# Retention/HGRN2 step on one core: both gates computed token-major in the value phase

## Chip, cores and metric

One of the eight cores of a Trainium2 chip runs the whole kernel. The metric is the device time of one execution in microseconds, as the median of the runs.

## What is computed

One step of a decoder layer for a prompt of 2048 tokens (model width 1024) and eight sample tokens with a past. The input is RMS-normalised and projected to eight groups of 512 columns: query, key, value and gate of the retention branch (rq, rk, rv, rg), and query, forget gate, value and gate of the HGRN2 branch (hq, hf, hi, hgate). Each branch has four heads of width 128. Cut to what matters:

```python
h = rmsnorm(x, norm_g)
rq, rk, rv, rg, hq, hf, hi, hgate = jnp.split(h @ w_in, 8, axis=-1)
rq, rk = rotary(rq, pos), rotary(rk, pos) * RET_DK ** -0.5
o_ret, s_ret_new = chunked_decay_recurrence(rq, rk, rv, log_gamma, s_ret)
o_ret = head_rmsnorm(o_ret, ret_g) * silu(rg)
logf = logaddexp(log(lb), log1p(-lb) + log_sigmoid(hf))
kin = (1 - lb) * sigmoid(-hf)
o_hg, s_hg_new = chunked_decay_recurrence(silu(hq), kin, hi, logf, s_hg)
o_hg = head_rmsnorm(o_hg, hg_g) * silu(hgate)
y = x + concat(o_ret, o_hg) @ w_out      # then the final rmsnorm
```

The recurrence is S_t = diag(f_t) S_{t-1} + k_t v_t^T, o_t = S_t^T q_t. It is worked in chunks of 128 tokens. The new states and the normalised y, for prompt and samples, are the outputs.

## The kernel before

Every float32 product is made of three fp32r products: each operand is split into a high part (a ScalarE copy) and a low part (a VectorE subtraction), in `hi_lo` (L105) and `split` (L109), and high*high, high*low and low*high are accumulated in PSUM. `three` (L303) issues them.

**The value phase.** The values of both branches are computed token-major (tokens on the partitions of the result). Eight pairs of 128-token chunks are worked through in `V_ORDER`. The first two pairs use the eight plain block products; pairs 2 to 7 use the Strassen-Winograd form with seven (`v_pair`, L307, with `PRODUCTS`). For it the weights are summed into T1 to T4 (`wv_comb`) and the tokens into S1 to S4 (`tok_ops`, L259, and `s_split`). `stats` (L222) gets the root mean squares of the tokens, `spread` (L245) brings them across the partitions with small matmuls (prs), and `tok_ops` scales the transposed tokens with them. Seven PSUM banks take the products in turn; ScalarE and VectorE combine them into four 128x512 results per pair (s, u, vo), which are stored to `v_dram`. The work for later pairs is hung behind the products of the current one (`after`).

**The main loop.** There are 16 units: two halves of the tokens, four heads, and for each head an HGRN unit and then a retention unit (`order`, L128). A unit projects a head's columns feature-major: retention q, k and gate (`ret_proj`, L619), HGRN forget gate, q and gate (`hgrn_proj`, L641, and `gate_steps`, L604). `seg_steps` (L564) cuts a projection into segments (512, 256 and 264 tokens in the first half, the eight sample tokens among them; 512 and 512 in the second) and each segment into four steps of six matmuls, followed by the evacuation. The gate is kept as g * silu(gate), features on the partitions (`gt`).

While a unit's projections run, the recurrence of the unit before it is worked off (`ret_rec`, L747; `hgrn_rec`, L781; `tail_steps`, L675). HGRN's steps are three rounds of small score matmuls (`scores0`, `scores`, `scores3`) with updates of k and q on VectorE (L811, L814) and copies on ScalarE (L821, L822) between them; then transposes of k (`kt`), the state sums (`uu`, L690 and L698), the outputs and their norm (`oo`, L705 to L715), and the transposes of the outputs (`tr`, L721), where the gate is multiplied in at L723 before the store to `o_dram`.

**What sets the order.** TensorE's order is the order of the program text; a planner writes it: `merge` (L1071) lays the recurrence's steps between the projection's steps in proportion to hand-written weights:

```python
steps = [(0.3, scores0), (2.3, lambda: scores(1)), (2.3, lambda: scores(3)), (2.3, scores3)]
steps += [(1.9, t["k0"]), (0.9, joined(t["u0"], t["k1"])), (1.1, t["u1"]),
          (1.2, joined(t["o0"], t["o1"])), (2.2, joined(t["t0"], t["t1"])), (0, last)]
```

A projection step weighs its columns/400. The other engines' orders are fixed by the compiler's scheduler; `behind` and `issue_after` tie some instructions to the place where they were written. `side_steps` adds the sample tokens' states (`d_load` to `d_mm`) and the sums of the output weights (`t_load_raw`, `t_sum`, `t_spool`).

**The output phase.** After the main loop the output projection runs, two chunks plainly and seven pairs in the seven-product form.

## Time and profile before

| | |
|---|---|
| median of 3 runs | 1065.55 us (1065.42 to 1066.16) |
| span of the profiled execution | 1062.5 us |
| ScalarE, GpSimd busy in it | 395.3 us, 115.8 us |
| mean granted TensorE clock | 0.999 |
| moved by DMA | 149.64 MB, mean 141 GB/s |
| on the chain that ended last: gate projections (pjg), output pairs (po), value pairs (pv) | 17%, 13%, 11% of the span |

The span runs from the first to the last instruction; the profiled execution is a single one, so its span is compared with the runs' median only through the difference of the two. The page gives the busy time of each engine, the chain of waits that ended last, and the costliest groups of instructions; other views are groups by shape, the timeline in order of time, and the busy time in chosen stretches. PE is TensorE, DVE VectorE, ACT ScalarE, POOL GpSimd. A name such as pjg is the tile that an instruction writes, and L578 the line of the program.

### The profile page before, as it was taken

The numbers are of one execution on the slowest core, as the hardware profiler recorded it, in microseconds if no ns is written. First come the engines' busy times: TensorE is split into PE (matmuls) and PEld (weight loads), VectorE is DVE, ScalarE is ACT, GpSimd is POOL, SyncE is SP. The second block draws the span as 40 slices with busy tenths as digits, with TensorE's granted clock in tenths as the row PEclk, the third lists the DMA queues.
The fourth block names the chain that finished last, engine by engine and source line by source line (L and its number), as shares of the span: only waits on it lengthen the run. The fifth ranks groups of instructions, "written<-read, shape, count | busy, mean of one in ns | idle before, by whom it ended". The sixth has DMA issues, their size and how long they took to land.

```text
span 1062.5 us, 21859 instructions
## 1 busy us (share of the span) xinstructions
PE 1050.9 (99%) x9107; PEld 899.6 (85%) x9107; DVE 733.6 (69%) x1271; ACT 395.3 (37%) x859; POOL 115.8 (11%) x218
## 2 busy tenths in 40 slices
PE   9999999999999999999999999999999999999997
PEld 7788888989989999998988888888788888788775
DVE  6886986594585567457977565746855687678785
ACT  7853323242432243333443323332423244333241
POOL 1110000001000010110110101011010103311122
PEclk9999999999999999999999999999999999999999
DMA  8664346422502240361654235126323337855642
GB/s 303 208 216 156 127 139 225 166 78 100 187 34 80 87 153 2 119 202 39 200 157 122 63 108 151 40 67 182 120 67 109 108 106 268 276 187 200 220 160 99
DMA packets 103890, 149.64 MB, mean 141 GB/s; under 512 B 5872, under 2 KB 69552, under 8 KB 103024
## 3 DMA queue, kind: packets, MB, share of 16 engines
q1 hardware_dynamic: 83888, 110.14, 32.9%
q0 software_dynamic: 6960, 25.24, 6.5%
q10 hardware_dynamic: 12944, 12.88, 3.5%
q8 instruction: 71, 1.16, 0.4%
q14 instruction: 27, 0.22, 0.1%
HBM read 109.86 MB, written 38.37 MB: 140 GB/s over the span
## 4 chain that ended last, share of the span: by engine, by line
PE 91%; DMA 3%; DVE 2%; ACT 2%; issue 1%; POOL 1%; SPq 0%; DVEq 0%; POOLq 0%; ACTq 0%
PE pjg L578 17%; PE po L305 13%; PE pv L305 11%; PE pjkr L578 9%; PE pjqr L578 8%; PE pjqh L578 8%; PE pjfh L578 8%; PE plh L841 2%; DMA xn<-in_x_prompt 2%; PE py L1231 1%; PE pur L690 1%; PE par L757 1%; PE por L705 1%; PE por L707 1%; PE poh L705 1%; PE puh L690 1%
## 5 line engine op out<-in xcount | busy, mean ns | idle before, releaser
L578 PE MATMUL pjg<-xh,w_h 128*128 128x512 f32 (+2 forms) x320 | 113.9, 356 | 0.0
L578 PE MATMUL pjg<-xh,w_l 128*128 128x512 f32 (+2 forms) x320 | 111.3, 348 | 0.0
L578 PE MATMUL pjg<-xl,w_h 128*128 128x512 f32 (+2 forms) x320 | 111.0, 347 | 0.0
L106 ACT ACTIVATE w_h<-wr 128x1024 fp32r<-128x1024 f32 x48 | 50.8, 1059 | 87.5 <-PE pjg L578 33.6
L107 DVE TENSOR_TENSOR w_l<-wr,w_h 128x1024 fp32r<-128x1024 f32 x48 | 58.6, 1222 | 23.3 <-ACT w_h L106 11.4
L578 PEld LDWEIGHTS pjg<-xh,w_l 128*128 128x128 f32 x320 | 60.2, 188 | 7.9
L578 PEld LDWEIGHTS pjg<-xh,w_h 128*128 128x128 f32 x320 | 60.3, 188 | 7.1 <-issue 0.4
L578 PEld LDWEIGHTS pjg<-xl,w_h 128*128 128x128 f32 x320 | 60.3, 188 | 6.7
L578 PE MATMUL pjqr<-xh,w_h 128*128 128x512 f32 (+2 forms) x160 | 58.2, 364 | 0.0
L578 PE MATMUL pjkr<-xh,w_h 128*128 128x512 f32 (+2 forms) x160 | 57.9, 362 | 0.0
L578 PE MATMUL pjfh<-xh,w_h 128*128 128x512 f32 (+2 forms) x160 | 57.4, 359 | 0.0
L821 ACT ACTIVATE kepth<-kh 128x1024 f32<-128x1024 f32 x24 | 25.5, 1062 | 85.6 <-DVE kh L811 85.6
L578 PE MATMUL pjqh<-xh,w_h 128*128 128x512 f32 (+2 forms) x160 | 56.6, 354 | 0.0
L578 PE MATMUL pjfh<-xh,w_l 128*128 128x512 f32 (+2 forms) x160 | 55.7, 348 | 0.0
L578 PE MATMUL pjkr<-xl,w_h 128*128 128x512 f32 (+2 forms) x160 | 55.5, 347 | 0.2 <-issue 0.2
L578 PE MATMUL pjkr<-xh,w_l 128*128 128x512 f32 (+2 forms) x160 | 55.6, 347 | 0.0
L578 PE MATMUL pjqh<-xh,w_l 128*128 128x512 f32 (+2 forms) x160 | 55.6, 347 | 0.0
L578 PE MATMUL pjqr<-xh,w_l 128*128 128x512 f32 (+2 forms) x160 | 55.6, 347 | 0.0
L578 PE MATMUL pjqr<-xl,w_h 128*128 128x512 f32 (+2 forms) x160 | 55.5, 347 | 0.0
L578 PE MATMUL pjqh<-xl,w_h 128*128 128x512 f32 (+2 forms) x160 | 55.5, 347 | 0.0
L578 PE MATMUL pjfh<-xl,w_h 128*128 128x512 f32 (+2 forms) x160 | 55.5, 347 | 0.0
L612 ACT ACTIVATE sg<-pjg 128x512 f32<-128x512 f32 (+2 forms) x40 | 20.4, 510 | 75.9 <-PE pjg L578 65.9
(851 smaller groups left out, 2819.5 us busy)
## 6 DMA issues: line engine op xcount, KB each, us to landing
wr<-in_w_in SPq DMA_DIRECT2D x48, 512.0 KB, 4.8
xn<-in_x_prompt SPq DMA_DIRECT2D x32, 256.0 KB, 3.0
v_dram<-vo SPq DMA_DIRECT2D x32, 256.0 KB, 2.8
v<-v_dram SPq DMA_DIRECT2D x16, 512.0 KB, 4.8
or<-o_dram SPq DMA_DIRECT2D x16, 512.0 KB, 5.8
xro<-in_x_prompt SPq DMA_DIRECT2D x14, 512.0 KB, 3.3
out_y_prompt<-xro POOLq DMA_DIRECT2D x13, 512.0 KB, 3.0
xr<-in_x_t SPq DMA_DIRECT2D x12, 512.0 KB, 4.4
```

The source lines that it names most:

```text
L106: act.activation(h, src, AF.Copy)
L107: dve.tensor_tensor(l, src, h.bitcast(F32), op=ALU.subtract)
L305: pe.matmul(ps, xx, ww, start=(first and n == 0), stop=(last and n == 2))
L578: pe.matmul(ps, ww[:, kk], x[:, k, b0 : b0 + n], start=(k == 0 and i == 0), stop=(k == KT - 1 and i == 2),)
L612: act.activation(sg[:, :n], ps, AF.Sigmoid)
L690: pe.matmul(pu[:, j], ksb[g][:, j], vcol(4 * g + j), start=True, stop=True)
L705: pe.matmul(po[:, j], A[:, c], vcol(c), start=True, stop=src is None)
L707: pe.matmul(po[:, j], qcol(c), src, start=False, stop=True)
L757: pe.matmul(pa[:, j], k[:, cc], q[:, cc], start=True, stop=True)
L821: act.activation(ss[:, 512:], k[:, :HALF], AF.Copy)
L841: pe.matmul(dst[32 * i : 32 * i + 32, c], kk, qq, start=True, stop=True)
L1231: pe.matmul(ps, o[:, kk], w[:, k % 4, i * 512 : (i + 1) * 512], start=(k == 0 and n == 0), stop=(k == KT - 1 and n == 2),)
```

## The change

The gate projections leave the main loop. After the value pairs, the value phase runs through all eight token pairs once more, with the gate columns as weights, in the seven-product form (`TOK`, pairs 8 to 15).

- The scaled tokens and their S sums are stored to DRAM in the first pass (`a_dram`, `s_dram`) and loaded in the second. The first two token pairs, which the first pass handles plainly, are scaled and summed in the second. `x_load` reads the scaled tokens too, so the scaling in `x_split` goes.
- The gate weights are loaded in pairs 3 to 6, multiplied with the sample tokens (`wg_decode`), summed (`w_sums`) and the sums stored (`g_sums`). In pair 7 each weight operand is fetched into the place of the value operand that was last used, and split over pairs 7 and 8.
- A pair now uses three PSUM banks: sums of products accumulate in the bank (`CHAIN`, sign of T4 turned), and copies of intermediate sums are taken by ScalarE.
- The gate results go through sigmoid and product, and to `g_dram`. The recurrence loads them like the values, and multiplies them in token-major, with the norm's factor: four operations of 128x128 in place of one of 128x512. The head norm's weight is applied after the transposes, by ScalarE in place of VectorE.
- The stores of the output weights' sums go from ScalarE's queue to GpSimd's, those of the new sample states from ScalarE's to SP's, one step later.

```diff
-        for g in ((RQ, RK, RG), (HF, HQ, HG))[ty]:
+        for g in ((RQ, RK), (HF, HQ))[ty]:
...
-    V_ORDER = [4, 5, 6, 7, 2, 3, 0, 1]
+    V_ORDER = [4, 5, 6, 7, 0, 1, 2, 3]
+    TOK = V_ORDER + [3, 2, 6, 7, 4, 5, 1, 0]
+    N_V = len(V_ORDER)
...
     def tok_ops(i):
         r0, r1 = xr[i]
...
+            if not spooled(i):
+                sp.dma_start(a_dram[TOK[i]][:, kk], r)
+        if spooled(i):
+            return
...
+        if i < N_V:
+            for n, t in enumerate(sraw[i]):
+                sp.dma_start(s_dram[TOK[i]][n], t)
...
+    CHAIN = [("A11", "B11", "a"), ("A12", "B21", "b"), ("S2", "T2", "a"), ("S1", "T1", "c"),
+             ("S3", "T3", "a"), ("S4", "B22", "c"), ("A22", "T4", "a")]
...
+        def emit(c, ty, ps, plus):
+            o = vq.tile([P, GW], F32, tag="vo", name=f"vo{i}{c}{ty}", bufs=3)
+            if plus:
+                dve.tensor_tensor(o, ps, box[plus], op=ALU.add)
+            elif not gate:
+                act.activation(o, ps, AF.Copy)
+            if gate:
+                src = o if plus else ps
+                sg = vq.tile([P, GW], F32, tag="sg", name=f"sg{i}{c}{ty}")
+                act.activation(sg, src, AF.Sigmoid)
+                dve.tensor_tensor(o, src, sg, op=ALU.mult)
+            v_out(int(gate), c, ty, o)
...
+        for n, (x, w, b) in enumerate(CHAIN):
+            first = b not in banks
+            if first:
+                banks[b] = bank([P, GW], f"pv{i}{b}")
+            ps = banks[b]
             for k in range(4):
-                three(ps, av(i, x, k), wv(w, k), k == 0, k == 3)
+                three(ps, av(i, x, k), wv(w, k), first and k == 0, k == 3, not first)
             if n == 0:
-                act.activation(keep("s1"), ps, AF.Copy)
+                keep("s1", ps)
             elif n == 1:
+                emit(ca, 0, ps, "s1")
             elif n == 2:
+                keep("u2", ps)
             elif n == 3:
+                keep("p5", ps)
             elif n == 4:
+                emit(ca + 1, 1, ps, "p5")
             elif n == 5:
+                emit(ca, 1, ps, "u2")
             else:
+                emit(ca + 1, 0, ps, None)
...
+    def wg_spool(k):
+        for op, r in w_sums(wr[k], wr[k + 4]):
+            sp.dma_start(g_sums[op][:, k], r)
...
+            if op in g_sums:
+                kk = slice(2 * n, 2 * n + 2)
+                r = Bop[op][1][:, kk].bitcast(F32)
+                pool.dma_start(r, g_sums[op][:, kk])
+            else:
+                r = rawp.tile([P, 2, GW], F32, tag="raw", name=f"wg{op}{n}")
+                kk = slice(k0 + 2 * n, k0 + 2 * n + 2)
+                sp.dma_start(r, a["w_g"][kk, :, c0 : c0 + GW].rearrange("k p n -> p k n"))
...
+        if 3 <= i < 7:
+            after[0] += [lambda k=i - 3: wg_load(k)]
+            after[3] += [lambda k=i - 3: wg_decode(k), lambda k=i - 3: wg_spool(k)]
...
-            dve.tensor_tensor(ob[g], po, rs.unsqueeze(2).to_broadcast([P, 4, P]), op=ALU.mult)
+            for j in range(4):
+                dve.scalar_tensor_tensor(
+                    ob[g][:, j], po[:, j], rs[:, j : j + 1], gcol(4 * g + j), op0=ALU.mult, op1=ALU.mult
+                )
...
-            dve.tensor_tensor(
-                ot, pt.rearrange("p a b -> p (a b)"), gt[:, g * 512 : (g + 1) * 512], op=ALU.mult
-            )
+            act.activation(ot, pt.rearrange("p a b -> p (a b)"), AF.Copy, scale=ng[:, hd : hd + 1])
...
-            act.dma_start(t_dram[x, n][:, :, k], y.bitcast(F32).rearrange("p (a b) -> p a b", a=2))
+            pool.dma_start(t_dram[x, n][:, :, k], y.bitcast(F32).rearrange("p (a b) -> p a b", a=2))
...
     def d_mm(hd):
         S, vb = dec["l", hd]
+        ty, h = divmod(hd, NH)
+        sp.dma_start(out[("new_ret_sample", "new_hgrn_sample")[ty]][0, :, h].rearrange("b d v -> d b v"), S)
```

More of the change, by code (lines that the diff above doesn't have):

```diff
@@ L304, in three @@
         for n, (xx, ww) in enumerate(((x[0], w[0]), (x[0], w[1]), (x[1], w[0]))):
-            pe.matmul(ps, xx, ww, start=(first and n == 0), stop=(last and n == 2))
+            pe.matmul(
+                ps, xx, ww, start=(first and n == 0), stop=(last and n == 2), skip_group_check=more
+            )
+    CHAIN = [("A11", "B11", "a"), ("A12", "B21", "b"), ("S2", "T2", "a"), ("S1", "T1", "c"),
+             ("S3", "T3", "a"), ("S4", "B22", "c"), ("A22", "T4", "a")]
     def v_pair(i, after):
-        ca = 2 * V_ORDER[i]
@@ L534, in step_kernel @@
+        if i in (7, 8):
+            for n, (_, op, _) in enumerate(CHAIN):
+                if (n + SPLIT_AT) // 7 == i - 7:
+                    after[(n + SPLIT_AT) % 7] += [lambda op=op: behind(lambda: wg_split(op))]
+        if i == n_tok - 1:
             after[0] += [w_load]
@@ L636, in ret_proj @@
             u[nm] = dst
-        u["gt"], g = gate_steps(half, 0, h)
-        steps.append(g)
         return u, steps
@@ L750, in ret_rec @@
         G = GAMMA[h] ** P
-        vcol = lambda c: v[0][:, c]
+        vcol, gcol = (lambda c, n=n: v[n][:, c] for n in range(2))
         def score(g):
@@ L921, in collect @@
         hd = ty * NH + h
[L922 removed]
+        for dst, key in ((dq, "q"), (dk, "k"), (df, "f")):
             if key in u:
@@ L1109, in unit @@
         box = []
-        steps.insert(len(steps) // 2, (0, lambda: box.append(values(half, ty, h))))
+        steps.insert(len(steps) // 2, (0, lambda: box.extend(values(n, half, ty, h) for n in range(2))))
         return steps, (u, box)
```

240 lines of the change are left out of this document (129 added, 111 removed).

## The prediction

> **What bounds the kernel now.** I read the page first, then the busy time by stage, then the chain that ended last in order of time.
>
> ```profile
> span 1062.5 us, 21859 instructions
> ## 1 busy us (share of the span) xinstructions
> PE 1050.9 (99%) x9107; PEld 899.6 (85%) x9107; DVE 733.6 (69%) x1271; ACT 395.3 (37%) x859; POOL 115.8 (11%) x218
> ```
>
> TensorE (PE) is idle for 1062.5 - 1050.9 = 11.6 us of the whole span. Nothing else comes near it: VectorE (DVE) is at 69%. So the time is the length of TensorE's instruction stream, and a change is worth what it takes out of that stream, less the stops that it brings. The stages show where a stop could come from. Columns: stretch, length, busy time of PE, PEld, DVE, ACT and POOL (instructions), granted clock, share of the DMA engines, GB/s.
>
> ```profile
> 61.85:174.30 112.45, 112.45 (x508) 93.05 (x507) 92.13 (x153) 41.42 (x68) 5.01 (x12) 1.00 0.50 165
> 0.00:20.00 20.00, 18.63 (x109) 14.88 (x109) 11.54 (x25) 13.50 (x27) 0.88 (x8) 1.00 0.88 316
> ...
> 655.40:701.80 46.40, 46.40 (x644) 39.12 (x642) 31.08 (x54) 16.05 (x37) 4.14 (x7) 1.00 0.25 71
> ```
>
> The first row is most of the value phase, the last one unit of the main loop: a retention unit of the second half of the tokens, whose projections run while the recurrence of the HGRN unit before it is worked off. In both TensorE never stops. VectorE is at 92.13/112.45 = 82% and 31.08/46.40 = 67%.
>
> **What TensorE is relieved of and given.** Matmuls are pipelined, so the busy mean of one (403 ns) is not its price. The price is the pitch in the chain.
>
> ```profile
> 61.85 19.09 PE pv L305 x84
> ...
> 185.14 5.44 PE pjg L578 x24
> 190.58 2.84 PE pjfh L578 x24
> ...
> 199.10 2.92 PE pjfh L578 x24
> ```
> ```profile
> L578 PE MATMUL pjg<-xh,w_h 128*128 128x512 f32 x192 | 77.4, 403 | 0.0
> ...
> L578 PE MATMUL pjg<-xh,w_l 128*128 128x264 f32 x64 | 18.3, 285 | 0.0
> L578 PE MATMUL pjg<-xh,w_h 128*128 128x256 f32 x64 | 18.2, 285 | 0.0
> ...
> L403 PE MATMUL pvd<-wvr,pk 128*8 128x256 f32 x64 | 3.8, 379 | 0.0
> ```
>
> Pitches: 5.44/24 = 0.227 us for a projection matmul of 512 columns, 0.118 for 256, 0.122 for 264, and 19.09/84 = 0.227 in the value phase. All eight gate projections (pjg) go. Each group exists for three products (high*high, low*high, high*low), so 3 x 192 x 0.227 + 3 x 64 x 0.118 + 3 x 64 x 0.122 = 130.6 + 22.7 + 23.4 = 176.7 us leave the stream. Eight token pairs of gate products come, of 7 x 12 = 84 matmuls each: 8 x 19.09 = 152.7 us. The gate of the eight sample tokens comes as a second set like pvd, 3.8 us by its row. The spread matmuls stay eight. Sum: 176.7 - 152.7 - 3.8 = **20.2 us less** for TensorE. Part of it is the seventh-for-eighth product; the rest is that the short 256- and 264-column matmuls cost more per column.
>
> **The cover that goes with the gate projections.** A unit's projections are also what TensorE does while VectorE and ScalarE work between two steps of the recurrence. The planner (merge) places the steps by weight over the projections, so with two projections in place of three every gap shrinks to two thirds. In the second half a unit now has 16 steps of six matmuls, 1.36 us each, planner weight 1.28, 20.48 in all. The HGRN steps weigh 14.5 together, so a step whose cumulative weight is c goes out at 0.98 x 20.48/14.5 = 1.38c. The step scores(3) (c = 4.9) follows the sixth matmul step, scores3 (7.2) the eighth: two steps or 2.72 us between them, where there were four. The two transposes (14.5) come two steps behind the outputs (12.3): again 2.72. What these gaps have to hold, from one unit of the second half:
>
> ```profile
> 669.96 0.70 PE L841 MATMUL plh<-qth,kh 128*32 128x16 f32 x62
> ...
> 674.44 0.68 DVE L814 TENSOR_TENSOR qth<-qth,fph 128x512 f32<-128x512 f32 x1
> ...
> 676.27 0.70 PE L886 MATMUL plh<-kepth 128*32 128x32 f32 x32
> ...
> 695.11 0.39 PE L707 MATMUL poh<-sth,qth 128*128 128x128 f32 x2
> ...
> 698.60 0.69 DVE L715 TENSOR_TENSOR obh<-poh,orsh 128x512 f32<-128x512 f32 x1 [1.08 <-POOL orsh L103]
> ...
> 700.80 1.03 PE L721 MATMUL poth<-ident,obh 128*128 128x128 f32 x8
> ```
>
> From the end of scores(3) (670.66) to the second update's end (675.12) it takes 4.46 us; TensorE came 5.61 us later and never noticed. scores3 begins with 0.63 us that need only the older copy (L886), so it must be ready after 2.72 + 0.63 = 3.35: short by 1.1 us. From the last output matmul (695.50) to the second normalised block (699.29) it takes 3.79 us.
>
> That second stretch also grows, because the gate is now applied there: one 128x512 product per block (L715) becomes four of 128x128 with a per-partition factor and a second tensor. The nearest row for one of those is the state update, which has the same operands:
>
> ```profile
> L698 DVE SCALAR_TENSOR_TENSOR sth<-sth,fph,puh 128x128 f32<-128x128 f32 x48 | 16.7, 347 | 9.7 <-PE puh L690 8.3
> ...
> L715 DVE TENSOR_TENSOR obh<-poh,orsh 128x512 f32<-128x512 f32 x16 | 11.1, 691 | 27.7 <-ACT jkh L711 16.9 <-POOL orsh L103 10.8
> ```
>
> 4 x 0.347 - 0.691 = +0.70 us a block, so the block is there 4.49 us after the outputs. The last transposes then end at about 4.49 + 0.28 = 4.77, against 2.72 + 1.03 = 3.75 without a wait: short by 1.0. So 2.1 us for each of the four HGRN recurrences of the second half, 8.4. In the first half the finer segments leave one step of 256 and four of 264 columns in both gaps, 0.71 + 2.92 = 3.63 us. There the same update was ready at 317.77, 4.90 us after its scores (312.87):
>
> ```profile
> 312.17 0.70 PE L841 MATMUL plh<-qth,kh 128*32 128x16 f32 x62
> ...
> 317.08 0.69 DVE L814 TENSOR_TENSOR qth<-qth,fph 128x512 f32<-128x512 f32 x1
> ```
>
> That is short by 4.90 - 0.63 - 3.63 = 0.6 at the scores, and by 4.77 - 3.63 - 1.03 = 0.1 at the transposes: 0.7 x 4 = 2.8. **Main loop: +11.2 us.** Bounds: 0, if VectorE takes the updates ahead of its other work, and 8 x 4.2 = 34, if it always takes them behind one whole rotary evacuation (four operations of the size of L715's, 2.8 us) and a weight split (one of twice that size, at most 1.4). I take the value between because the two measured stretches have that queue as it runs. The gate also lay between the last q evacuation and the next unit's first scores. What stands there now is the transposes (1.03) and one step (1.36), against a sigmoid and two operations of L715's size, about 2 us: cost 0; if those do not cover, 0.5 a unit. Retention recurrences have wider gaps (weights 1.3 and 1.7 of 5.0): 0.
>
> ScalarE takes the transposed blocks in place of VectorE and loses the gate's sigmoids and weight splits; at 16.05/46.40 it stays covered. The stores moved off its queue are costed at nothing. On SP the new-state stores go out one step later, already computed, ahead of weight loads that have a projection's lead (11 us). On POOL a store of the output weights' sums stands ahead of the norm's two operations; if its split is late, it holds them by that split, 1.4 us, and it falls in units with wide gaps.
>
> **The value phase.** It gets eight more pairs, three new kinds of stores, and sums that accumulate in the bank in place of separate banks. So the evacuation of one product must be over before the next but one begins, one product (12 x 0.227 = 2.73 us) later. Now it is far later than that, unnoticed:
>
> ```profile
> 89.21 0.39 PE L305 MATMUL pv<-T1h,s31l 128*128 128x512 f32 x1
> ...
> 99.40 0.68 DVE L334 TENSOR_TENSOR vo<-pv,u 128x512 f32<-128x512 f32 x1
> ```
>
> The fifth product ends at 89.6 and its sum runs at 99.4, behind the next pair's token work. The change relieves that queue: of seven VectorE evacuations a value pair keeps three, the copies go to ScalarE, and the output buffers go from two to three. Walking the queue from the spread (about 1 us after the second product), through eight scalings, two splits, four sums, the first S split and, in pairs 3 to 6, four weight sums, I estimate the add at about 12.3 us after the second product; TensorE asks for it after four more products, a spread and sample matmuls, 10.9 + 1.4. I take 0.5 us for each of six pairs, **+3 us**; bounds 0 and 7 a pair (9.8 less 2.73), 42 us.
>
> At the end, the last recurrence's block is already waited for, so its 0.7 us comes half on top: **+0.5**.
>
> ```profile
> 914.61 0.63 PE L721 MATMUL potr<-ident,obr 128*128 128x128 f32 x4 [1.00 <-DVE obr L715]
> ```
>
> Sum: -20.2 + 11.2 + 3 + 0.5 = -5.5, a span of 1057.0 us. The median of the runs, 1065.55, is 3.05 above the span, so **1060 us**. Anything within 0.2% (2.1 us) counts as no change; that is about what a measurement can tell here.
>
> **Rivals.** (a) The cover is enough: VectorE orders its queue well, both stalls stay under 3 us together, and the relief arrives nearly whole: 1065.6 - 20.2 + 2 = 1047. For it: VectorE is idle a third of the unit above. Against: the 2.72 us gaps.
>
> (b) Slower: the HGRN recurrence becomes the bound of the retention units. TensorE's part of such a unit falls from 46.4 to 46.4 - 48 x 0.227 = 35.5 us; VectorE's 31.08 hardly falls, so it would be up to 88% busy in a chain of steps that each wait for TensorE, ScalarE and GpSimd in turn. From a mean stop of (20.2 - 3.5)/8 = 2.1 us per HGRN recurrence on, the change loses. At 4.2 us, a whole rotary evacuation and a split ahead of the chain in every unit, it is 1065.6 - 20.2 + 34 + 3.5 = 1083.
>
> (c) Slower: DMA in the value phase. It moved 165 GB/s; pairs 3 to 5 now move 7 MiB each (token load, statistics load, gate weights, value stores, and stores of scaled tokens, S sums and weight sums) in 20.5 us with their spread and sample matmuls, 358 GB/s. The best stretch above moved 316 at 88% of the engines. At 316 those three pairs take 23.2 us, 2.7 more each, and pair 7, which fetches the second weight set, some 5; with the copies stuck behind late loads this puts 8 + 5 on the forecast: 1073. Against: the buffers let transfers lag by a pair.
>
> [...] No stretch of this trace reaches 358.
>
> That the gates leave the main loop but TensorE does not get shorter cannot be: the pitches are its own.
>
> **How the numbers follow.** Forecast 0.37 (0.07 of it ends within 0.2%), (a) 0.24, (b) 0.22, (c) 0.17 (0.03 of it within 0.2%). Faster 0.30 + 0.24 = 0.54, same 0.10, slower 0.22 + 0.14 = 0.36. The likeliest case alone spans 1051 to 1066. The range, 1046 to 1080, takes in (a), (c) and the milder half of (b).
>
> **What would show it.** Right: no pjg; 8 more pv pairs of 19.1 us; retention units of 36 to 38 us, with TensorE's waits on VectorE at L886/L891 and before the transposes in the second half. Wrong: retention units at 35.5 with no idle (a), at 39 or more (b), or idle PE in pairs 2 to 8 with ScalarE or the adds waiting for DMA (c).

## The result and the profile after

The changed kernel takes **1103.5 us** (median; 1100.7 to 1105.4) against 1065.5 before: a ratio of 1.035, 95% interval 1.033 to 1.037. The forecast was 1060, with 1046 to 1080 as its range. It was slower by 38 us where 5 us less were expected.

The head of the page after; in the prediction the same line gave TensorE 1050.9 us and 99%.

```profile
span 1103.5 us, 21912 instructions
...
PE 1056.8 (96%) x8883; PEld 883.1 (80%) x8883; DVE 760.3 (69%) x1363; ACT 458.0 (42%) x957; POOL 133.3 (12%) x243
```

TensorE is now idle for 1103.5 - 1056.8 = 46.7 us, where it was 11.6. VectorE is still at 69%: no other engine became the bound in the sum. The mean granted clock fell from 0.999 to 0.983, so a busy PE also hides slower matmuls: a 512-column projection matmul was busy for 0.63 us at 445.6 us, at a clock of 0.50, and for 0.39 at 449.7, at 1.00.

The prediction's stream, 1062.5 - 20.2 = 1042.3 us with no stop beyond those of before, is missed by 61.2 us. By stages, from the first pjfh and py matmuls of the trace: the value phase ends at 343.5 us where 174.1 + 156.5 = 330.6 was due (**+12.9**); the main loop takes 572.6 us where 706.6 - 176.7 = 529.9 was due (**+42.7**; the units below sum to 42.6, the figure in the expectations); the output phase takes 187.4 us instead of 181.8 (**+5.6**).

What TensorE waited for in the main loop (columns: tile and line, releaser, us in total, times, longest):

```profile
engine line waited for: us in total, times, longest us
PE potr L803 <- DVE obr L795: 6.1, 3, 2.6
PE plh L921 <- issue: 4.2, 3, 2.0
PE pah L940 <- DVE qh L744: 3.9, 3, 1.7
PE plh L921 <- DVE qth L894: 2.7, 2, 2.2
PE poth L803 <- DVE obh L795: 2.2, 4, 1.2
PE plh L921 <- ACT kepth L902: 2.0, 2, 1.6
```

Before, no such line in the whole kernel was over 1.1 us. (Line numbers are now those of the changed kernel: L795 is the norm with the gate, L803 the transposes of the outputs, L921 the small score matmuls, L940 the first of them, L744 the q evacuation, L894 and L902 the update of q and the copy of it that the scores read. potr and poth are the transposes of the retention and the HGRN recurrences. "issue" means that the engine waited for nothing that the profile shows.)

The value phase, in four pairs and one retention unit of the second half (columns as in the prediction's stages):

```profile
78.00:98.70 20.70, 20.70 (x105) 16.45 (x104) 14.53 (x25) 8.17 (x16) 0.01 (x1) 1.00 0.89 325
119.50:142.60 23.10, 21.47 (x106) 16.26 (x105) 14.47 (x25) 8.57 (x17) 1.08 (x3) 1.00 0.89 311
184.30:209.20 24.90, 21.24 (x85) 16.74 (x84) 21.12 (x22) 16.93 (x22) 0.54 (x1) 0.93 0.95 365
209.20:228.30 19.10, 19.10 (x86) 15.81 (x85) 8.68 (x12) 7.55 (x11) 0.00 (x0) 1.00 0.53 174
661.83:700.90 39.07, 37.50 (x603) 31.14 (x602) 29.86 (x60) 14.47 (x35) 4.57 (x8) 1.00 0.13 44
```

Pair 3 has its 84 matmuls, spread and sample matmuls without a stop; pair 5 has the same work and 1.6 us of idle, behind token statistics whose load ScalarE waited for (the row below); pair 8, the first of the gates, loses 3.7 us of idle and then some clock; pair 9 is the bare pitch of 19.09. In the retention unit TensorE stops for 1.57 us.

```profile
123.32 0.63 ACT L242 ACTIVATE xn<-xn 128x512 f32<-128x512 f32 x1 [2.82 <-DMA xn<-in_x_prompt]
```

### The profile page after: what moved, and what is told of

Same layout as the page of the kernel before. It is cut to its first block, busy times and chain, and to the rows that moved or that the text cites. A ratio compares the mean times of both kernels' runs of the same rounds, so it can differ in the third digit from the quotient of the medians.

```text
span 1103.5 us, 21912 instructions
## 1 busy us (share of the span) xinstructions
PE 1056.8 (96%) x8883; PEld 883.1 (80%) x8883; DVE 760.3 (69%) x1363; ACT 458.0 (42%) x957; POOL 133.3 (12%) x243
## 3 DMA queue, kind: packets, MB, share of 16 engines
q8 instruction: 70, 1.15, 0.4%
## 5 line engine op out<-in xcount | busy, mean ns | idle before, releaser
L676 PE MATMUL pjqr<-xh,w_h 128*128 128x512 f32 (+2 forms) x160 | 62.5, 391 | 1.6 <-DVE qh L744 0.8
L111 DVE TENSOR_TENSOR w_l<-wr,w_h 128x1024 fp32r<-128x1024 f32 x32 | 39.1, 1223 | 33.6 <-ACT w_h L110 11.3
L110 ACT ACTIVATE w_h<-wr 128x1024 fp32r<-128x1024 f32 x32 | 33.9, 1059 | 66.9 <-DMA wr<-in_w_in 19.6
L901 ACT ACTIVATE kepth<-kh 128x1024 f32<-128x1024 f32 x24 | 25.4, 1060 | 87.1 <-DVE kh L891 87.1
L676 PE MATMUL pjkr<-xl,w_h 128*128 128x512 f32 (+2 forms) x160 | 55.5, 347 | 0.0
L676 PE MATMUL pjfh<-xl,w_h 128*128 128x512 f32 (+2 forms) x160 | 55.5, 347 | 0.0
L676 PE MATMUL pjqh<-xl,w_h 128*128 128x512 f32 (+2 forms) x160 | 55.5, 347 | 0.0
L111 DVE TENSOR_TENSOR xl<-xr,xh 128x1024 fp32r<-128x1024 f32 (+1 forms) x38 | 40.1, 1066 | 11.9 <-ACT xh L110 11.9
L891 DVE TENSOR_TENSOR kh<-kh,fph 128x512 f32<-128x512 f32 x48 | 33.4, 695 | 14.9 <-PE plh L921 14.6
L110 ACT ACTIVATE xh<-xr 128x1024 fp32r<-128x1024 f32 (+1 forms) x38 | 34.5, 930 | 20.9 <-DVE xr L273 18.5
L676 PEld LDWEIGHTS pjqr<-xh,w_h 128*128 128x128 f32 x160 | 32.0, 200 | 8.4 <-issue 2.8
L795 DVE SCALAR_TENSOR_TENSOR obh<-poh,orsh,g 128x128 f32<-128x128 f32 x64 | 18.0, 343 | 27.0 <-POOL orsh L107 19.6
L676 PEld LDWEIGHTS pjqr<-xh,w_l 128*128 128x128 f32 x160 | 32.2, 201 | 4.7
L790 ACT ACTIVATE jkh<-poh 128x128 f32<-128x128 f32 x64 | 17.7, 277 | 41.7 <-PE poh L786 40.3
```

The lines of the kernel that those rows point to most:

```text
L110: act.activation(h, src, AF.Copy)
L111: dve.tensor_tensor(l, src, h.bitcast(F32), op=ALU.subtract)
L676: pe.matmul(ps, ww[:, kk], x[:, k, b0 : b0 + n], start=(k == 0 and i == 0), stop=(k == KT - 1 and i == 2),)
L790: act.activation(jk, po[:, j], AF.Square, accum_out=ms[:, j : j + 1])
L795: dve.scalar_tensor_tensor(ob[g][:, j], po[:, j], rs[:, j : j + 1], gcol(4 * g + j), op0=ALU.mult, op1=ALU.mult)
L891: dve.tensor_tensor(kv[:, :, 0, :], kv[:, :, 0, :], two[:, :, 1:2].to_broadcast([P, nb, b]), op=ALU.mult)
```

## The main loop unit by unit

Each unit's length, from the first matmul of its projections in the trace to the first of the next unit's, against its length before less the gate projection (11.2 us in the first half, 10.9 in the second). "no shared buffer" is the experiment `inplace`, below.

```
unit, fills the gaps of     due    after   excess   no shared buffer
1  R, HGRN recurrence       36.0   43.6    +7.6     37.7
2  H, retention             31.3   34.9    +3.6     31.2
3  R, HGRN                  35.6   37.2    +1.6     36.5
4  H, retention             31.3   34.6    +3.3     31.2
5  R, HGRN                  35.6   37.2    +1.6     36.4
6  H, retention             31.2   33.8    +2.6     31.2
7  R, HGRN                  36.3   41.4    +5.1     45.7
8  H, retention             31.3   32.0    +0.7     32.0
9  R, HGRN                  35.7   37.9    +2.2     37.9
10 H, retention             32.3   33.5    +1.2     32.9
11 R, HGRN                  35.3   40.6    +5.3     38.2
12 H, retention             32.4   32.7    +0.3     32.8
13 R, HGRN                  36.1   41.3    +5.2     42.2
14 H, retention             32.4   33.4    +1.0     33.5
15 R, HGRN                  34.7   36.0    +1.3     36.2
```

The excess is not spread evenly, as one term for each recurrence would have it.

## Experiments

**Is it the cover?** `keep_proj` keeps the gate projections in the main loop and throws their result away; `keep_ret` and `keep_hgrn` do so in the retention or the HGRN units alone.

```diff
-        for g in ((RQ, RK), (HF, HQ))[ty]:
+        for g in ((RQ, RK, RG), (HF, HQ, HG))[ty]:
...
+        steps.append(gate_steps(half, 0, h))     # retention units; hgrn_proj likewise
```

> The kernel after the change, with the eight gate projections also kept in the main loop, their result thrown away: TensorE's stream is 176.7 us longer, the cover is what it was before. Theory 'cover': all 42.6 us by which the main loop was longer than its stream vanish: 1103.5 + 176.7 - 42.6 = 1238. Theory 'late buffers': the part that hangs on the moved stores (about 19 us) stays: 1257. If the main loop's loss is neither: 1280.

> The kernel after the change, with thrown-away gate projections in the retention units alone, which cover the HGRN recurrences. The stream is 88.35 us longer: 1191.9 if nothing is covered. By the stops in the trace after the change, those in retention units (368 to 376, 594 to 597, 627, 663, 739, 807 to 815, 889 us) and the half clock behind them are 21 us: 1171. By rival (b) of the prediction (HGRN recurrences alone bind): nearly all of the 37 us that full cover gave back, 1155.

> The same with the thrown-away gate projections in the HGRN units alone, which cover the retention recurrences. Stream 88.35 us longer, 1191.9 if nothing is covered. By the stops in the trace (440, 513, 584, 712, 850 us and the half clock): 13 us back, 1179. By the prediction's term 'retention recurrences 0': 1191.9.

Measured: 1243.2, 1172.2 and 1177.1 us. 176.7 us of stream cost 139.7, so full cover takes back **37.0 of the 42.7 us**. The halves take back 88.35 - 68.7 = 19.7 (retention units) and 88.35 - 73.5 = 14.8 (HGRN units). So the HGRN recurrences alone do not explain it. (`keep_hgrn` has 11.9 us of "issue" stops, which are looked into below, so its half may understate the cover.) With full cover TensorE waited in the main loop only here:

```profile
engine line waited for: us in total, times, longest us
PE plh L937 <- ACT kepth L918: 6.4, 1, 6.4
PE plh L937 <- issue: 0.7, 2, 0.5
```

The one long wait falls in unit 1, which takes 55.5 us where it took 47.2 before. What it waits for is a buffer, not the recurrence's own chain (ScalarE in `keep_proj`, then in the kernel before):

```profile
386.82 1.06 ACT L110 ACTIVATE w_h<-wr 128x1024 fp32r<-128x1024 f32 x1 [5.33 <-DMA t_dramh<-wos01h]
388.73 0.66 ACT L918 ACTIVATE kepth<-qth 128x512 f32<-128x512 f32 x1
```
```profile
217.32 1.06 ACT L106 ACTIVATE w_h<-wr 128x1024 fp32r<-128x1024 f32 x1 [3.05 <-DMA t_dramh<-wos01h]
```

A weight split waits until a store has landed and freed its buffer, and the copy for the scores stands behind that split. The kernel before had the same wait, but its copy (at 212.66 us) stood ahead of the split, and TensorE did not stop.

`before_nogate` asks the opposite: the old kernel with the gate a constant tile and no gate projections.

```diff
-        u["gt"], g = gate_steps(half, 0, h)
-        steps.append(g)
+        u["gt"] = gts                            # memset once; hgrn_proj likewise
```

> The kernel before, without the eight gate projections (the gate is a constant tile): the main loop alone loses its cover, and nothing moves to the value phase, no store changes its queue, and the norm keeps one product a block. TensorE's stream falls by 176.7 us, to 888.8 with no stops. Theory 'cover': most of the main loop's 42.6 us appear here too, less the 0.7 us a block of the norm: 920 to 930. By the prediction's own working (1.1 us at the scores and 0.3 at the transposes of the second half, 0.6 in the first): 897. Theory 'late buffers' or the norm's products: 889 to 895.

Measured: 957.7 us (952.0 to 961.8), 68.9 above its stream and 28 above the range that was expected. Its main loop takes 583.3 us, 53.4 more than due; the rest is mostly in the output phase, where the first sums wait 10.4 us for the outputs' load and TensorE 9.0 behind them. Taking the gate projections away is enough for a loss of the main loop's size. The changed kernel's is 10.7 us smaller; which of its other edits won that back (a transpose evacuation less on VectorE, among others) no run separates.

**The queue of the moved stores.** In units 2, 4 and 6 TensorE stopped before the transposes of a retention recurrence, for which the prediction had costed 0. In unit 2 (timelines of TensorE, ScalarE, VectorE and GpSimd, and one row of the DMA issues):

```profile
443.10 1.10 PE L803 MATMUL potr<-ident,obr 128*128 128x128 f32 x4 [2.61 <-DVE obr L795]
```
```profile
433.99 1.06 ACT L110 ACTIVATE w_h<-wr 128x1024 fp32r<-128x1024 f32 x1 [5.90 <-issue]
434.96 0.26 ACT L790 ACTIVATE jkr<-por 128x128 f32<-128x128 f32 x1
```
```profile
437.04 1.22 DVE L111 TENSOR_TENSOR w_l<-wr,w_h 128x1024 fp32r<-128x1024 f32 x1 [5.08 <-DMA t_draml<-wos10l]
438.19 1.12 DVE L795 SCALAR_TENSOR_TENSOR obr<-por,orsr,g 128x128 f32<-128x128 f32 x4
```
```profile
428.81 0.69 POOL L1033 DMA_DIRECT2D t_draml<-wos10l  x1 [0.56 <-DVE wos10l L111]
434.25 0.68 POOL L1033 DMA_DIRECT2D t_draml<-wos11l  x1 [4.04 <-issue]
```
```profile
t_draml<-wos10l POOLq DMA_DIRECT2D x1, 512.0 KB, 8.2
```

The low part w_l of the next projection's weight waits 5.08 us until a store of the output weights' sums has landed, 8.2 us after its issue: both use the same three buffers. The squares (jkr) and the normalised block (obr) stand behind that split on their engines. First suspect: GpSimd's queue, to which these stores had moved.

```diff
-            pool.dma_start(t_dram[x, n][:, :, k], ...)
+            act.dma_start(t_dram[x, n][:, :, k], ...)
```

> The stores of the output weights' sums go back from GpSimd's queue to ScalarE's; all else as after the change. Theory 'late buffers' (these stores leave GpSimd's queue microseconds late, so the split buffers come free late and hold ScalarE and VectorE in front of the recurrences): the stops of TensorE at the start of the second unit (1.6 and 2.2 us) and before the transposes of units 3, 5 and 7 (2.6, 2.0, 1.5 us) go, and with them the stretches of half clock behind them (about 1.7 us each), some 18 us: 1085. Theory 'cover' (the recurrence is too long for the projections that are left, whatever the queues): the same stops stay, 1103. If ScalarE is held by issuing the stores itself: slower than 1103.

> The kernel after the change with both kinds of stores moved back to ScalarE's queue, the new-state stores also back to the earlier step. Prediction's step 'moved stores cost nothing': 1103 to 1105, as with the first kind alone (1104.3). If the state stores on SP hold the weight loads behind them: faster than 1101.

Measured: 1104.3 (1103.2 to 1107.4) and, with both kinds of stores back, 1101.4 us (1098.9 to 1108.0). The stop in unit 2 was even 3.9 us. The queue is not the cause; my theory falls, and the prediction's "moved stores at nothing" stands.

**The shared buffers.** `inplace` leaves the queue and splits the sums in their own raw tiles.

```diff
-        for x, y in zip("hl", split((t, ra)[n]...)):          # wh, wl: the weights' buffers
+        src = (t, ra)[n]
+        hh = rb if n == 0 else rawp.tile([P, 2, GW], F32, tag="raw", ...)
+        hi_lo(hh.bitcast(F32R), src.bitcast(F32R), src)
+        for x, y in zip("hl", (hh, src)):
```

> The kernel after the change, with the sums of the output weights split in the raw tiles themselves, not in the three buffers that the projections' weights use (the stores stay on GpSimd's queue). Theory 'shared buffers' (in the shortened units the weight split for the next projection waits until a store of these sums has landed and frees its buffer, and the squares and the normalised block queue behind it on ScalarE and VectorE): the stops before the transposes at 440, 513 and 584 us (2.6, 2.0, 1.5) go, with the half clock behind them: between 6 and 11 us less, 1093 to 1098. Theory 'chain' (the retention recurrence itself is too long for two projections): the stops stay, 1103.

Measured: **1088.6 us** (1086.3 to 1092.5), 14.9 less, more than expected, ratio to before 1.022 (1.020 to 1.025). Units 2, 4 and 6 come down to their due lengths and unit 1 loses 5.9 us of its excess. In unit 2 the weight splits now wait under a microsecond and the transposes run without a stop:

```profile
425.83 1.23 DVE L111 TENSOR_TENSOR w_l<-wr,w_h 128x1024 fp32r<-128x1024 f32 x1 [0.86 <-ACT w_h L110]
427.44 1.23 DVE L111 TENSOR_TENSOR w_l<-wr,w_h 128x1024 fp32r<-128x1024 f32 x1 [0.38 <-ACT w_h L110]
429.95 1.13 DVE L795 SCALAR_TENSOR_TENSOR obr<-por,orsr,g 128x128 f32<-128x128 f32 x4 [1.28 <-POOL orsr L107]
```
```profile
433.12 1.04 PE L803 MATMUL potr<-ident,obr 128*128 128x128 f32 x8
```

So the gate projections had covered not only the recurrence but also the landing of these stores. The two scores waits of unit 1 (plh for kepth 1.6 us and for qth 2.2) are gone as well. Of the main loop's excess 28.2 us are left in `inplace`: its waits sum to 18.0 us (8.7 of them "issue", 4.0 pah), some 4 are half clock behind them, and about 6 are placed by no view.

**The half clock.** In the changed kernel the granted clock mostly fell to 0.50 after stops of 1.5 to 3.5 us, in eight stretches of 3.4 or 6.8 us (the first at 199.1 us, behind the 3.48 of pair 8). `dummy` fills three of the stops with matmuls of ones, ahead of the transposes.

```diff
+            if half == 0 and hd < 3 and g == 0:
+                for j in range(12):
+                    pe.matmul(pt[:, j % 4], ones, ones, start=True, stop=True)
```

> The kernel after the change, with twelve matmuls of ones (about 1.6 us) ahead of the transposes of the first half's retention recurrences of heads 0 to 2, written where the transposes write afterwards. Theory 'clock' (a stop of 1.5 us or more halves the granted clock for about 3.4 us, which costs 1.7 us on top of the stop): the three stops shrink to under 1.1 us, the half clock behind them at 444, 516 and 588 us does not come, 3 x 1.7 = 5 us less: 1098. If the clock falls for another reason: 1103.5, with the same low clock. If the added matmuls only queue in front: 1108.

Measured: 1103.6 us, no change, although the clock stayed at 1.00 in all three places. From the second block of transposes to the next round of scores (busy time by stage, after and `dummy`):

```profile
443.10:451.65 8.55, 8.28 (x150) 5.93 (x150) 7.37 (x17) 2.60 (x4) 1.01 (x2) 0.80 0.38 125
```
```profile
442.23:450.10 7.87, 7.11 (x150) 5.08 (x150) 7.35 (x17) 2.57 (x4) 1.19 (x2) 1.00 0.41 135
```

Of 1.7 us of lost clock 0.7 shows, and the idle share of the stretch grows from 0.27 to 0.76 us: VectorE is busy for 7.4 us either way, and TensorE at full speed waits for it. The second of the three places gives 0.7 as well. That the whole did not change is not for want of this gain. The filler was larger than planned:

```profile
438.29 2.84 PE L804 MATMUL potr<-ones 128*128 128x128 f32 x24
```

It took 2.84 us instead of 1.6 and put the second block of transposes 0.7, 0.4 and 1.7 us later in its unit, which gave the gain back: from a unit's start to the next scores it is 42.1, 41.7 and 41.9 us after and 42.2, 41.5 and 42.0 in `dummy`. So the half clock cost less here than the clock that it took (0.7 of 1.7 us), but the run does not show that it cost nothing.

**The first scores and the stops of "issue".** `inplace_w` raises the planner's weight of the first HGRN scores on top of `inplace`.

```diff
-        steps = [(0.3, scores0), (2.3, lambda: scores(1)), ...
+        steps = [(1.5, scores0), (2.3, lambda: scores(1)), ...
```

> The kernel 'inplace' (1088.6 us) with the planner's weight of the first HGRN scores raised from 0.3 to 1.5, so that they follow two projection steps instead of one behind the last q evacuation. Theory 'cover' at this place (the gate projection used to stand between that evacuation and the first scores): the stops before pah (0.85, 1.25, 1.68 us and the half clock behind the last) go: 1083 to 1086. Rival: the gaps later in the recurrence shrink by a twelfth each and what is won there is lost: 1088.6 or more.

Measured: 1098.0 us (1097.5 to 1099.5), 9.4 **worse**. The waits of pah for the q evacuation went from 4.0 us to 0.3, but the stops of "issue" rose from 8.7 us to 11.8, and the later steps lost their room: plh waited 6.5 us for VectorE and ScalarE, where it had waited 1.2. In `inplace` the longest of the "issue" stops:

```profile
577.52 0.65 PE L921 MATMUL plh<-qth,kh 128*32 128x16 f32 x57
582.02 0.30 PE L921 MATMUL plh<-qth,kh 128*32 128x16 f32 x5 [3.85 <-issue]
```
```profile
DMA  9999999999999999999999999999999999999883
GB/s 336 326 315 338 346 365 358 354 356 354 358 383 383 430 356 344 344 340 383 371 449 332 422 348 455 385 397 373 373 354 383 381 348 358 342 315 301 274 252 100
```

The second fence is the DMA between 570 and 580 us. TensorE stops in the midst of a burst, at about the same matmul in each kernel (after 57 here, after 57 to 60 in the changed kernel and in the experiments below that have it). The page after has a queue of instructions:

```profile
q8 instruction: 70, 1.15, 0.4%
```

70 packets of 1.15 MB together, 16.4 KB each: TensorE has 2 x 8883 instructions, about 254 a packet, and by that one round of scores (128 matmuls and 128 weight loads) uses up a packet. By its counts the queue is TensorE's: `before_nogate` with 8147 matmuls has 64 such packets, `keep_proj` with 9843 has 77. Three runs moved or removed data traffic, all on `inplace`:

```diff
 inplace_vq:    values and gates of a unit loaded at a fifth of it instead of half
 inplace_nox2:  if blk == 2: pool.memset(r, 0.1); return r        # in place of its eight loads
 inplace_nodec: pool.memset(S, 0.1); pool.memset(vb, 0.1)         # in place of the samples' loads
```

> 'inplace' (1088.6 us) with one edit: the values and gates of a unit are loaded at a fifth of it instead of half. Theory 'late instructions': the stops of 'issue' at 575 to 582, 724 and 804 us (8.7 us together, and two half clocks) depend on what the DMA engines carry at that time, so they change place or shrink with the loads: 1082 to 1087, or more than 1089 if the loads now meet the weight loads. Theory 'density': the same stops at the same bursts, 1088.6 within 1.

> 'inplace' (1088.6 us) without the transfers of the third token block (2 MB in the seventh HGRN and retention unit; GpSimd writes a constant instead, so that block's output is not computed). The instructions are the same but for the ten transfers. Theory 'late instructions' (TensorE's instructions come in packets of 16 KB through the same DMA engines, and behind 340 to 400 GB/s of data a packet lands after the burst of small matmuls has used up the one before): the stops at 575 and 578 us (0.8 and 3.9) and the half clock behind them (1.9) go, the later ones stay: 1082 to 1084. Theory 'density': the stop within the burst at 578 stays, 1088.

> 'inplace' without the sixteen loads of the sample states and sample values in the second half (8 MB; GpSimd writes constants instead, so the samples' output is not computed). Theory 'late instructions': the stops of issue at 724 and 804 us (1.2 and 1.7, with 1.7 of half clock) shrink, that at 578 stays: 1084 to 1086. Theory 'density': all stay, 1088.

`inplace_vq`, 1093.0 us (1085.7 to 1098.4): the stop at the same burst is 4.36 us, others came up at 653 and 796 us; nothing won, and a wide spread. `inplace_nox2`, 1085.3 us (four of its executions 1083.9 to 1086.8; the profiled one 1093.8, with a stop of 2.6 us at 383 us, far from the edit): the stop is 1.47 us where it was 3.85, and unit 7 takes 40.3 us where it took 45.7. `inplace_nodec`, 1084.0 us (1082.3 to 1085.5): its stop in unit 7 is still 3.8 us, but from 715 to 830 us only this is left of issue, where `inplace` had 2.9 in two:

```profile
PE plh L921 <- issue: 0.3, 1, 0.3
```

The expected 1084 to 1086 us of `inplace_nodec` came, the 1082 to 1084 of `inplace_nox2` (its trace has eight transfers less, not ten) were missed by 1.3. Each removal shortened the stops near its own transfers, but one profiled execution does not prove it: in `inplace_nox2` the stops at 725 and 805 us, far from its edit, shrank too (2.9 us to 1.4). The packets themselves show more. Times in us of single packets of this queue, from the traces (the data rate is from the beginning of the packet before to the end of this one):

```
kernel          packet before  this packet         TensorE      stop   data moved
                began          began to ended      goes on             meanwhile
inplace         573.35         579.72 to 580.65    582.02       3.85   325 GB/s
inplace_vq      570.56         577.34 to 578.21    579.67       4.36   330 GB/s
inplace_nox2    581.77         585.49 to 586.52    588.03       1.47   245 GB/s
after           592.13         595.66 to 596.61    597.99       1.42   141 GB/s
inplace_w       376.64         380.18 to 381.10    382.56       1.65    18 GB/s
before_nogate   583.79         587.21 to 588.14    589.56       1.97    20 GB/s
```

Of the 82 stops of "issue" over 0.25 us in all the traces here, 81 end 1.2 to 1.7 us after such a packet has ended. So these stops are late instructions; that part is shown. Two things go with their being late. No two packets of a trace began less than 3.2 us apart (3.38 before, 3.41 after), and a burst needs the next one after about 1.3 us (one round of 128 matmuls took 1.27 us, from 669.39 us in the kernel before): TensorE stopped for 1.65 and 1.97 us with 18 and 20 GB/s moving (the last two rows). With more data in flight the distance was longer. At the burst of the seventh unit two packets follow each other in thirteen of the kernels, 3.4 to 4.4 us apart at 140 to 275 GB/s (six of them) and 6.1 to 7.0 us apart at 325 to 365 (seven). So "density" and "late instructions" both hold, and the 1.47 us that stay in `inplace_nox2` are what a distance of 3.7 us leaves.

**The value phase.** `no_switch` computes the gate products with the value weights, without fetching or splitting the second set; `no_sdram` computes the token sums S again instead of storing and loading them.

```diff
-            for n, (_, op, _) in enumerate(CHAIN):
-                after[n] = [lambda op=op: wg_fetch(op)] + after[n]       # no_switch; wg_split too
...
-            for n, t in enumerate(sraw[i]):
-                sp.dma_start(s_dram[TOK[i]][n], t)                       # no_sdram; its loads too
```

> The kernel after the change without the change of the weight set: the gate products use the weights of the value products again (so the gates are not the reference's), and the eight pieces of the second set are neither fetched nor split. Theory 'switch' (pair 8 is 5.9 us over its pitch because the second set arrives at the rate of the DMA engines, and 1.7 of that is half clock): pair 8 takes 19.04 us, 1097 to 1098. If the token loads alone hold pair 8: it stays at 22 us or more, 1101 or more. Pairs 5 and 6 (23.05 and 22.73 us, against 20.77 in pairs 3 and 4) stay as they are.

> The kernel after the change, with the four S sums of the tokens computed again for the gate products instead of stored in the value pass and loaded: 6 MB less stored, 6 MB less loaded, about 2.8 us more VectorE work in each of six gate pairs. Theory 'DMA' (the value phase's 13 us over its stream come from transfers that arrive late): the stops at 55, 125, 148 and 195 us (1.7, 0.7, 1.1, 3.5) shrink, at least those before 160 us, 3 to 8 us less: 1096 to 1100. If the transfers are not what ends these stops: 1103.5; if VectorE is late instead in the gate pairs: slower.

Measured: 1096.2 us (1094.0 to 1099.4) with pair 8 at 19.04 us instead of 24.9 and pairs 5 and 6 unchanged (22.7 each); 1100.4 us (1095.7 to 1101.5) with pairs 5 and 6 at 20.79 but pair 3 at 23.6. Each removal helps in its own pairs. In pair 3 of `no_sdram` TensorE waits 1.9 us for VectorE's sum (vo), the evacuation that the prediction had priced; why it comes late there is open, and the 3 us that `no_sdram` wins lie within the spread of the runs. In pair 8 (TensorE, VectorE, ScalarE, then the stretch 184 to 199 us with its 416 GB/s):

```profile
198.84 0.61 PE L320 MATMUL pv8a<-T3h,s70h 128*128 128x512 f32 x1 [3.48 <-ACT u L334]
```
```profile
195.00 0.69 DVE L339 TENSOR_TENSOR vo<-pv8b,s 128x512 f32<-128x512 f32 x1 [1.89 <-DMA v_dram<-vo]
```
```profile
195.78 0.63 ACT L345 ACTIVATE sg<-vo 128x512 f32<-128x512 f32 x1 [4.04 <-DVE vo L339]
196.32 1.99 ACT L110 ACTIVATE B22h<-wgB 128x1024 fp32r<-128x1024 f32 x2
198.21 0.58 ACT L334 ACTIVATE u<-pv8a 128x512 f32<-128x512 f32 x1
```
```profile
184.30:198.80 14.50, 11.06 (x49) 8.82 (x47) 11.43 (x12) 9.93 (x14) 0.54 (x1) 1.00 1.04 416
```

What TensorE waited for was not a weight: a sum waits until a store of values has landed, ScalarE's sigmoid waits for the sum, and the copy u that TensorE needs stands behind the sigmoid and a weight split. `no_switch` takes away the traffic and the splits of the second set together, so their shares are not separated.

**Together.** `best1` joins `inplace`, `no_sdram`, the weight of 1.5 and ten filler matmuls in pair 8; `best2` retimes loads and sample steps as well; `best3` is `best2` without the weight and the filler.

> 'inplace' with three edits: the S sums computed again instead of stored and loaded (measured alone: 3 us less), the weight of the first HGRN scores 1.5, and ten matmuls of ones (1.1 to 1.3 us) ahead of the fifth product of the ninth pair, where TensorE stops for 2.7 to 3.5 us at the change of the weight set. If the three add up: 1088.6 - 3 - 3 to 4, and 1.7 for a half clock that does not come behind the stop, where TensorE bounds what follows: 1080 to 1082. If the half clock costs nothing there either: 1082 to 1084.

> 'best1' with transfers and decode steps retimed: values and gates loaded at a fifth of a unit instead of half, three of the decode heads earlier or a unit later, the output phase's first sums later. Theory 'late instructions' (the stops of 'issue' inside the small score matmuls, 3.9, 1.2 and 1.7 us and their half clock, fall where the DMA engines are full): with the loads elsewhere they shrink, 4 to 8 us less than 'best1'. Theory 'density' (too many small matmuls in too short a time, whatever the DMA): they stay, within 2 us of 'best1'.

> 'best2' (1090.0 us) with the weight of the first HGRN scores back at 0.3 and without the added matmuls. The weight alone cost 9.4 us on 'inplace'; if it does so here: 1080 to 1082. If the retimed loads had already taken the stops that the weight made: 1088 to 1090.

Measured: 1095.0, 1090.0 and 1096.3 us. None adds up. The filler in pair 8 (2.4 us instead of the 1.1 to 1.3 expected) only moved the stop from the fifth product to the last (2.5 us), which waits for a sum behind T4's split on VectorE. `best2` against `best1` agrees with "late instructions" (9.5 us in plh alone to 3.8), but `best3` missed by 15 us: 11 us of issue, 5.0 before pah. Without the higher weight and the filler the same retiming hurts; no setting of weights and loads found here wins everywhere. `inplace`, at 2.2% above before, is not reliably beaten by any version that computes everything, and none reaches the kernel before.

## Why the prediction was wrong, point by point

- **The bound and the stream: right.** TensorE stayed the bound; gate pairs 9, 10 and 13 to 15 take 19.04 us each (19.09 forecast); units 2, 4 and 6 of `inplace` take 31.2 where 31.3 was due. The 20.2 us are there, and are spent.
- **The main loop, +11.2 with 34 as its bound: the step that failed, +42.7.** Within it:
  - *"Retention recurrences have wider gaps: 0."* Units 2, 4 and 6 lost 9.5 us to them. The width was right (`inplace` has no wait there); what ran in the gaps was not the chain alone but a weight split that waited for a store, 5.1 us in unit 2. The prediction did ask whether the sums could hold GpSimd, by 1.4 us, and not whether their buffers could hold the next weights. The same wait took 5.9 us in unit 1, in an HGRN recurrence; together 15.4 us, where `inplace` is 14.9 faster.
  - *1.1 us at scores3 and 1.0 at the transposes of the second half.* scores3 showed no wait in the trace after; the transposes waited 1.2 us in unit 7 and 0.33 in three units of the second half. For those gaps the estimate was too high.
  - *The last q evacuation, 0 to 0.5 a unit.* pah waited 3.9 us in three units (1.0, 1.3, 1.7): on VectorE two splits of the output weights' sums stand ahead of the evacuation in unit 1, sample steps and splits of the next weights in the two units of the second half.
  - *Not in the working at all:* late instructions, 5.0 us of issue stops after (4.2 in plh, 0.8 at a projection), 0.2 before, 0.7 in `keep_proj`. The gate projections had spread the bursts of small matmuls over time. Nor is the half clock in it, six stretches of the main loop with 23.9 us at 0.50 together.
- **The norm's factor, +0.70 a block:** right. obh's row is 343 ns for one (0.347 assumed).
- **The moved stores at nothing:** right for the queues (1101.4 and 1104.3 with them back).
- **The value phase, +3 with 42 as its bound: 12.9.** Not VectorE's own queue, which the prediction had walked, but the transfers: pairs 5 and 6 took 2.3 and 2.0 us more than pairs 3 and 4, pair 8 5.9 more than its pitch. That is the mechanism of rival (c), but not its places: it gave 8 us to pairs 3 to 5, where pairs 5 and 6 took 4.3, and some 5 to pair 7, where pair 8 took 5.9. Its 8 + 5 = 13 beside the measured 12.9 is luck, the more so as it came on top of the forecast's 3. (c) alone would have been 1073.
- **The rate of 358 GB/s.** Rival (c) needed it for three pairs and priced them by the 316 of its best 20 us. 358 was no ceiling here: the trace after moved 416 over 14.5 us, and over 5 us even the trace before moved 411 (890 to 895 us). The pairs 5 and 6 were late at 311 GB/s all the same, with the engines busy at 0.89 and 0.87: no rate alone gave the price. By the trace's own 316 GB/s the prediction had 23.2 us for such a pair, and they took 23.05 and 22.73; but pairs 3 and 4 moved 325 and 335 GB/s and took 20.77.
- **Rival (b), 1083:** half right. It gave HGRN recurrences 34 us (8 x 4.2), and by `keep_ret` they cost 19.7; the other 14.8 lay behind retention recurrences, for which it had nothing. The sign that was named for it, retention units of 39 us or more, came in four of the eight (40.6 to 43.6), not in the others (36.0 to 37.9).
- **The end, +0.5: 5.6.** The prediction read the block of the last retention recurrence (potr, 0.3 us after); the wait came at the last HGRN unit. Its outputs waited twice, behind sums that wait for the stored outputs, and the clock was 0.50 for 6.8 us behind that:

```profile
927.41 1.01 PE L803 MATMUL poth<-ident,obh 128*128 128x128 f32 x4 [1.98 <-DVE obh L795]
930.35 1.25 PE L803 MATMUL poth<-ident,obh 128*128 128x128 f32 x4 [1.93 <-DVE obh L795]
```
```profile
926.31 0.69 DVE L1353 TENSOR_TENSOR oS<-or 128x512 f32<-128x512 f32 x1 [3.74 <-DMA or<-o_dram]
```

  Their place in the order is a share of the output stage, and the unit ahead of it is 9.6 us shorter (45.6 to 36.0). That this is why they come too early is argued; no run moves them alone.
- **The likeliest case** assumed that each stop could be costed from its own chain. The span was missed by 1103.5 - 1057.0 = 46.5 us: 42.7 - 11.2 = 31.5 in the main loop, 12.9 - 3 = 9.9 in the value phase, 5.6 - 0.5 = 5.1 at the end. The profiled execution took 1105.4 us, 1.9 above the median of its runs.

## What to carry to other kernels

Work on the bounding engine that looks replaceable can also cover what showed as almost no wait while it stood there: here the landing of stores whose buffers others need (8.2 us after the issue in unit 2; 14.9 us of the time, by `inplace`), and the arrival of that engine's own instructions (0.2 us of issue stops before, 5.0 after). Before such work is taken out of a loop, list for each shared buffer who frees it and how late, in the shortened unit and not only in the old one. A cheap test comes first: take the work out alone, or put it back as waste; here either run would have given the sign before the second half of the change was written.

## What the runs showed of the hardware that was not expected

- TensorE's instructions arrive in packets of 16.4 KB through the DMA engines, in these traces never less than 3.2 us apart and 6 to 7 us apart with 325 to 365 GB/s of data in flight. A burst of small matmuls uses one up in 1.3 us and then stopped for up to 4.4 us; it went on 1.2 to 1.7 us after the next packet had ended. Executions of one such kernel differed by 1% (`inplace_vq`, 1085.7 to 1098.4 us), where the kernel before, beside it, took 1065.6 to 1067.4; that the late instructions make this spread is likely, not shown.
- The granted clock halved for 3.4 or 6.8 us behind stops of 1.5 to 3.9 us, but not always: it stayed at 1.00 behind stops of 1.25, 1.42 and 1.67 us in the changed kernel, of 1.93 us in `inplace` and of 2.80 us in `before_nogate`.
- The lost clock was not all lost time: of 1.7 us behind a stop 0.7 showed in the next 8 us (after against `dummy`), because VectorE was busy for 7.4 of them and TensorE at full speed waited for it.
